# MLP of a two-layer decoder: weight blocks placed behind the features, eight loaded at once, sums and row scaling moved earlier

## The chip, the cores and the metric

The kernel runs on one core of a Trainium2 chip. The metric is the device time of one execution in microseconds (us), and the number quoted for a kernel is the median of several runs. TensorE (PE) does the matmuls, VectorE (DVE), ScalarE (ACT) and GpSimd (POOL) the elementwise work. SyncE (SP) and POOL issue the DMAs that bring weights from HBM; a DMA issued by POOL can add to what lies in its target instead of replacing it (here: accumulating DMA).

## The reference

A decoder trunk of two layers over 512 rows of width 1024, in float32. Layer 0 mixes rows with gated linear attention, layer 1 with stick-breaking attention; behind each mixer stand a norm, an MLP of width 4096 and another norm. Cut to what matters:

```python
def sq_relu_mlp(x, w_up, w_down):
    h = jax.nn.relu(x @ w_up)
    return (h * h) @ w_down

for layer in range(2):
    mix = gla_mixer(h, ...) if layer == 0 else stick_breaking_attention(...) @ sb_w_o
    h = layer_norm(ALPHA * h + mix, ln_g[layer, 0], ln_b[layer, 0])
    h = layer_norm(ALPHA * h + sq_relu_mlp(h, mlp_w_up[layer], mlp_w_down[layer]),
                   ln_g[layer, 1], ln_b[layer, 1])
```

`layer_norm` takes a row's mean and variance, then multiplies by a gain vector `ln_g` and adds a bias vector `ln_b`.

## The kernel before

**Precision.** Every float32 operand is split into a rounded part `hi` (written by ACT, L70 for weights and L98 for features) and the rest `lo` (DVE, L72 and L99). A product takes three matmuls: hi·hi, hi·lo, lo·hi. So each weight block of 128x1024 costs one ACT and one DVE instruction before PE can use it.

**Seven products.** Each 2x2 block product is done with seven block products instead of eight. This needs sums of features (`T`, `tmp` and `s`, DVE lines L725, L840 and L855) and sums of weight blocks. Half of the block sums come for nothing, as accumulating DMAs on POOL (L748, `Blocks.more`); the rest are a DVE addition (L773, `Blocks.sum`) or a DMA of one block onto another (POOL, L771).

**The stages.** The mixer of layer 0 ends in its output projection, the generator `seven` (L341 and on, matmuls at L392). It gives back control after each finished row tile, and `finish` norms that tile: mean and variance on DVE (L177, L182), reciprocal root on POOL (`ve`, `rs`, L183 and L184), centring on DVE (L190), transposes on PE (L267) and the gain and bias in the transposed form on ACT (L270). Four row tiles `h304` to `h307` hold the residual rows. Then `mlp(0, ...)` runs, then the values' projection and the attention of layer 1, its projection `project`, and `mlp(1, ...)`, which ends in the last norm and the store.

**The MLP.** The width of 4096 is cut into four chunks (`NC`). A chunk is an `up` half of seven steps (matmuls at L922, 256 columns each) and a `down` half of seven steps (L973, 512 columns). An object `Step` holds a step's weight blocks and feature operand; `run_all` makes both two steps ahead. `between()` runs inside a step after its matmuls are issued, and is where the next steps' operands are written. `read` takes a step's result from PSUM: in an up step by an ACT copy (L933) or a DVE sum (L938), in a down step by the DVE sums of `Rows.add` (L167, L169). `AHEAD` lists a half's eight weight blocks (four, each in two halves `h`): two plain ones and two that also get an accumulating DMA.

**The first up of an MLP.** Its first two steps use plain pieces (`raw`), loaded ahead. Of its eight blocks, four (layer 0: with their accumulating DMAs) are loaded on SP before the first row tile is normed, and the last four are loaded by POOL (L895) in `rest()`, behind a small POOL copy `pin` (L956) that reads the last row tile's `rs`. In layer 1 two of the accumulating DMAs are issued there too. So POOL's order there is: last `rs`, `pin`, those, then the loads.

**Rows' scaling.** The residual rows get gain and bias on their own, off the path: `times` (L199, DVE, by `lng`) for the four tiles during steps 4 and 5 of the first up and steps 0 and 1 of the first down, `plus` (L202) during the second up. `lng` and `lnb` are loaded on SP by `lnvec` before the output projection in layer 0, and before `finish` in layer 1.

**What sets the order.** Each engine runs its queue in program order. A scheduler places the instructions; those in `keep(...)` (`tc.keep_in_program_order`) stay where the code has them. A load into a pool's slot waits until the former use of that memory is over. In the MLP's pool the block slots (tag `B`) lie at the bottom, where layer 0 had gating tiles and layer 1 the attention's query and key tiles, and the feature tiles (tag `s2`) above them.

Of the kernel before, what the change touches and what calls it, by code (L numbers as in the profile page):

```python
# [8 lines left out]
F32 = mybir.dt.float32  # L9
# [25 lines left out]
def yoco_kernel(ctx: ExitStack, tc: tile.TileContext, x, gla_w_in, gla_w_a2, gla_b_a, gla_norm_g,  # L35
# [298 lines left out]
    def seven(a1, a2, weights, pool, hs, fresh, norms=(), mid=None, begun=None):  # L334
# [9 lines left out]
        bs = []  # L344
# [8 lines left out]
        for h in range(2):  # L353
            four_b = []
            for k, j, other in ((1, 1, (0, 1)), (0, 1, (0, 0)), (0, 0, None), (1, 0, None)):
                b = pool.tile([P, 1024], F32, tag="B", bufs=8, name=nm("B"))
                nc.sync.dma_start(out=b.rearrange("p (a b) -> p a b", a=2), in_=weights(k, h, j))
                if other:
                    more(b, h, *other)
                four_b.append(b)  # L360
            bs.append(four_b)

        def split_b(i):
            got = []
            for h in range(2):
                hi, lo = split_tile(bs[h][i], 2)
# [42 lines left out]
        third = split_a(s1), split_b(1)  # L409
# [303 lines left out]
    vec, vcols = lnvec(0, 0), lncols(0, 0)  # L713
# [79 lines left out]
    def mlp(l, hT, late, vec, done, ready=None):  # L793
# [11 lines left out]
        def operand(a, apart=False):  # L805
# [5 lines left out]
            else:  # L811
                us = [unit(F32R)]
                put(us[0][:, :, LO], us[0][:, :, HI], a)
# [6 lines left out]
        def steps(a11, a12, a21, a22, weights, part, read, order, by=(), plain=None, ops=None, after=None, late_sums=False):  # L820

            made, t = [], []
            hold = keep if after else lambda ins: ins

            def blocks(k=0, j=0, first=False, sums=None):
                def make():
                    if first and not made:
                        made.append(Blocks(mlp_, weights, order, by))
# [6 lines left out]
                    return made[0].pieces(k, j, keep if after and (k, j) == (0, 1) else lambda ins: ins)  # L835
# [22 lines left out]
            makes = [lambda: operand(a11()), lambda: operand(a12()), sum3, sum4, sum5, sum6, lambda: operand(a22())]  # L858
# [19 lines left out]
            def step(n):  # L878
                banks, opens, closes, (i, j), first, make = table[n]

                def go(between=lambda: None):
                    for s in part(me.a, me.b, banks, opens, closes, n):
                        if s == 1:
                            between()
                        yield from read(s, banks, i, j, first, n)

                me = Step(go, make, makes[n])
                if after and n == 0:

                    def rest():  # L890
                        after()
                        if late_sums:
                            for h in range(2):
                                made[0].more(made[0].b[1, 1], (0, 1), h, keep)
                        made[0].load(AHEAD[:2], lambda **to: keep(nc.gpsimd.dma_start(**to)))  # L895

                    me.rest = rest
                if after and n == 3:
# [640 lines left out]
```

## Time and profile before

| what | value |
|---|---|
| median of 3 runs | 1125.41 us (1121.54 to 1128.05) |
| the profiled execution's own time | 1123.68 us |
| its span | 1122.0 us |
| PE busy | 1090.2 us (97%) |
| DVE busy | 903.0 us (80%) |
| ACT busy | 669.7 us (60%) |
| POOL busy | 179.6 us (16%) |
| read from HBM | 176.52 MB, 160 GB/s over the span |
| mean granted clock of PE | 0.991 |

Time outside the span is 1.7 us. Row formats in what follows: a line of the timeline gives start, duration (both in us), engine, line, operation, output<-input, shape, count, and in brackets the time that the engine stood idle just before and what ended it. A line of the table by stages gives, for one stretch, each engine's busy time, then PE's granted clock (1.00 is full), the busy share of the 16 DMA engines and GB/s. Stretches of the run: the output projection of layer 0 from 155 to 218 us, its MLP to about 525, values and attention to about 735, the second projection to 785, the last MLP to 1122.

### The profile page before, as it was taken

Reading aid. Unit: us, or ns where it says so; the run is one execution under the profiler, and the core shown is the slowest. Engines: PE = TensorE matmul, PEld = TensorE weight load, DVE = VectorE, ACT = ScalarE, POOL = GpSimd, SP = SyncE. Lnnn points to the kernel's source line nnn. Section 1 sums busy time; section 2 is a strip of 40 time slices with the busy share of each in tenths; the row PEclk is TensorE's granted clock in tenths of the full one; section 3 lists DMA queues with packets and bytes.
Section 4 is the critical chain, followed back from the end, with each engine's and each line's share of the span. In section 5 each row is a group of like instructions: output and inputs, shape, how many; then the busy total and the mean of one; then the engine's idle time right before and its main releaser. Section 6 shows DMA issues by size and latency. Waiting matters only on the chain. (4 is left out here: it accounts for less than half of the span.)

```text
span 1122.0 us, 16726 instructions
## 1 busy us (share of the span) xinstructions
PE 1090.2 (97%) x6463; PEld 940.2 (84%) x6463; DVE 903.0 (80%) x1087; ACT 669.7 (60%) x963; POOL 179.6 (16%) x213
## 2 busy tenths in 40 slices
PE   9999999999899999999899999999898999999997
PEld 7888878898698898897688777788896998988985
DVE  4488638988989878878887896688789889788787
ACT  4455426676467466565674776776675565574654
POOL 1011210312102101111204001212211022011012
PEclk9999999999999999999999999999899999999998
DMA  7262394778859949866748425356987699599483
GB/s 221 73 187 64 118 240 124 187 226 231 218 148 229 232 144 245 205 171 149 219 83 213 125 76 127 101 111 169 244 208 215 148 247 228 139 221 235 145 223 75
DMA packets 120867, 195.43 MB, mean 174 GB/s; under 512 B 13978, under 2 KB 38938, under 8 KB 120788
## 3 DMA queue, kind: packets, MB, share of 16 engines
q1 hardware_dynamic: 90580, 127.78, 35.4%
q0 software_dynamic: 27744, 61.87, 30.3%
q10 hardware_dynamic: 2464, 4.72, 1.2%
q8 instruction: 51, 0.84, 0.3%
q14 instruction: 28, 0.23, 0.1%
HBM read 176.52 MB, written 3.15 MB: 160 GB/s over the span
## 5 line engine op out<-in xcount | busy, mean ns | idle before, releaser
L72 DVE TENSOR_TENSOR lo<-B,hi 128x1024 fp32r<-128x1024 f32 x206 | 247.3, 1220 | 71.9 <-ACT hi L70 69.6
L70 ACT ACTIVATE hi<-B 128x1024 fp32r<-128x1024 f32 x206 | 212.9, 1054 | 154.2 <-DVE B L773 73.5
L973 PE MATMUL ps<-hi,T 128*128 128x512 f32 x896 | 281.3, 391 | 7.9 <-ACT T L98 3.9
L922 PE MATMUL ps<-T,hi 128*128 128x256 f32 x1280 | 235.6, 286 | 5.1 <-DVE T L99 3.9
L922 PEld LDWEIGHTS ps<-T,hi 128*128 128x128 f32 x1280 | 201.9, 194 | 8.7 <-DVE T L99 4.9
L973 PEld LDWEIGHTS ps<-hi,T 128*128 128x128 f32 x896 | 167.4, 188 | 47.2 <-DVE T L99 5.6
L922 PE MATMUL ps<-T,lo 128*128 128x256 f32 x640 | 181.1, 286 | 1.0 <-DVE lo L72 1.0
L973 PE MATMUL ps<-lo,T 128*128 128x512 f32 x448 | 174.9, 391 | 2.4 <-DVE lo L72 2.4
L922 PEld LDWEIGHTS ps<-T,lo 128*128 128x128 f32 x640 | 123.2, 194 | 2.1 <-DVE lo L72 1.9
L70 ACT ACTIVATE hi<-raw 128x1024 fp32r<-128x1024 f32 x88 | 91.1, 1057 | 45.2 <-PE ps L94 9.3
L72 DVE TENSOR_TENSOR lo<-raw,hi 128x1024 fp32r<-128x1024 f32 x86 | 102.8, 1217 | 18.0 <-ACT hi L70 17.6
L973 PEld LDWEIGHTS ps<-lo,T 128*128 128x128 f32 x448 | 84.2, 188 | 20.8 <-DVE lo L72 4.1
L922 PE MATMUL ps<-A,hi 128*128 128x256 f32 x512 | 93.1, 284 | 0.6 <-ACT hi L70 0.6
L922 PEld LDWEIGHTS ps<-A,hi 128*128 128x128 f32 x512 | 80.1, 192 | 0.8 <-ACT hi L70 0.8
L93 PE MATMUL ps<-T,hi 128*128 128x512 f32 (+1 forms) x200 | 79.7, 399 | 0.4 <-DVE k L99 0.4
L98 ACT ACTIVATE T<-s 128x1024 fp32r<-128x1024 f32 (+1 forms) x52 | 51.5, 994 | 46.6 <-DVE s L855 39.2
L748 POOL DMA_DIRECT2D B<-in_mlp_w_down_dram x32 | 38.5, 1203 | 244.6 <-DVE lo L72 103.5
L95 PE MATMUL ps<-T,lo 128*128 128x512 f32 (+1 forms) x200 | 76.5, 383 | 0.0
L94 PE MATMUL ps<-T,hi 128*128 128x512 f32 (+1 forms) x200 | 76.3, 382 | 0.0
L169 DVE TENSOR_TENSOR h<-h,ps 128x512 f32<-128x512 f32 x108 | 71.0, 679 | 1.7 <-PE ps L973 1.7
L922 PE MATMUL ps<-A,lo 128*128 128x256 f32 x256 | 72.2, 284 | 0.0
L99 DVE TENSOR_TENSOR T<-s,T 128x1024 fp32r<-128x1024 f32 (+1 forms) x52 | 59.2, 1138 | 6.7 <-ACT T L98 6.7
(234 smaller groups left out, 1888.0 us busy)
## 6 DMA issues: line engine op xcount, KB each, us to landing
B<-in_mlp_w_down_dram SPq DMA_DIRECT2D x64, 512.0 KB, 5.2
B<-in_mlp_w_up_dram SPq DMA_DIRECT2D x56, 512.0 KB, 4.9
B<-in_mlp_w_up_dram POOLq DMA_DIRECT2D x40, 512.0 KB, 9.3
B<-in_mlp_w_down_dram POOLq DMA_DIRECT2D x32, 512.0 KB, 9.4
raw<-in_mlp_w_up_dram SPq DMA_DIRECT2D x24, 512.0 KB, 4.6
B<-B POOLq DMA_DIRECT2D x24, 512.0 KB, 5.3
raw<-in_gla_w_in_dram SPq DMA_DIRECT2D x20, 512.0 KB, 3.7
raw<-in_mlp_w_down_dram SPq DMA_DIRECT2D x16, 512.0 KB, 8.9
```

The costliest lines, as they stand in the source:

```text
L70: keep(nc.scalar.activation(hi, raw, AF.Copy))
L72: keep((on or nc.vector).tensor_tensor(lo, raw, hi.bitcast(F32), op=ALU.subtract))
L93: keep(nc.tensor.matmul(ps, lhsT=a[0], rhs=b[0], start=first, stop=False))
L94: keep(nc.tensor.matmul(ps, lhsT=a[0], rhs=b[1], start=False, stop=False))
L95: keep(nc.tensor.matmul(ps, lhsT=a[1], rhs=b[0], start=False, stop=last))
L98: keep(nc.scalar.activation(hi, ps, AF.Copy))
L99: keep((on or nc.vector).tensor_tensor(lo, ps, hi.bitcast(F32), op=ALU.subtract))
L169: nc.vector.tensor_tensor(h, h, ps, op=op)
L748: keep(nc.gpsimd.dma_start(out=got[h].rearrange("p (a b) -> p a b", a=2), in_=self.w(other[0], h, other[1]), accum_op=ALU.add))
L922: nc.tensor.matmul(to, lhsT=b[k][x][:, fs], rhs=a(k)[:, y], start=opens and f % 2 == 0 and (k, x, y) == (0, 0, LO), stop=closes and (k, x) ...
L973: nc.tensor.matmul(banks[s], lhsT=a(k)[:, x][:, P * s:P * s + P], rhs=b[k][y], start=opens and (k, x, y) == (0, LO, 0), stop=closes and (k ...
```

## The change

1. `seven` allocates and loads its eight blocks in the order in which the products use them (`b11`, then `b22`, `b21`, `b12`, both halves each), instead of one half after the other. The splits of the third product (`b12`) are kept in program order.
2. In the MLP's pool the two feature tiles of the first chunk come first (`sq0`), so that the block slots lie behind them, over other former tiles: in layer 0 blocks of the output projection, in layer 1 the attention's work tiles. The mask `low` moves to another pool.
3. The first up's eight blocks are all loaded on SP when they are made, those with accumulating DMAs first. `rest()`, `pin` and the POOL loads of L895 are gone; all four accumulating DMAs of a layer are issued among the norms' POOL work.
4. Both halves of the first block sum (L773) are done in `between()` of step 0, that is during the last tile's norm. Step 0's ACT copies are kept in order at step 1's `between()`.
5. The four `times` come at steps 2, 4, 5 and 6 of the first up, none in the down half. `lng` and `lnb` are loaded in `run_all`, behind the eight blocks.
6. Two operands are pinned in program order: that of `a22` in the first up, and that of `a11` in the downs of later chunks.

The diff, cut to its core (the line numbers of the changed kernel differ a little: L348 for L347 and so on, L922 becomes L920, L840 L843, L855 L858, L938 L937):

```diff
-        for h in range(2):
-            four_b = []
-            for k, j, other in ((1, 1, (0, 1)), (0, 1, (0, 0)), (0, 0, None), (1, 0, None)):
-                b = pool.tile([P, 1024], F32, tag="B", bufs=8, name=nm("B"))
+        for i in (2, 3, 0, 1):
+            for h in range(2):
+                bs[h][i] = pool.tile([P, 1024], F32, tag="B", bufs=8, name=nm("B"))
+        for i, k, j, other in ((2, 0, 0, None), (0, 1, 1, (0, 1)), (3, 1, 0, None), (1, 0, 1, (0, 0))):
+            for h in range(2):
+                b = bs[h][i]
                 nc.sync.dma_start(out=b.rearrange("p (a b) -> p a b", a=2), in_=weights(k, h, j))
                 if other:
                     more(b, h, *other)
...
-        third = split_a(s1), split_b(1)
+        third = split_a(s1), split_b(1, keep=tc.keep_in_program_order)
...
-    vec, vcols = lnvec(0, 0), lncols(0, 0)
+    vcols = lncols(0, 0)
...
+        sq0 = [four(), four()]
...
-                        made.append(Blocks(mlp_, weights, order, by))
+                        made.append(Blocks(mlp_, weights, AHEAD[2:] + AHEAD[:2] if first_up else AHEAD, by))
...
-                        yield from read(s, banks, i, j, first, n)
+                        if first_up and n == 0:
+                            me.read = lambda: read(s, banks, i, j, first, n)
+                        else:
+                            yield from read(s, banks, i, j, first, n)
...
-                    def rest():
-                        after()
-                        if late_sums:
-                            for h in range(2):
-                                made[0].more(made[0].b[1, 1], (0, 1), h, keep)
-                        made[0].load(AHEAD[:2], lambda **to: keep(nc.gpsimd.dma_start(**to)))
-
-                    me.rest = rest
-                if after and n == 3:
-                    me.sum = lambda: (minus_a11(), made[0].sum((0, 0), (1, 1), 0))
+                if first_up and n == 3:
+                    me.sums = lambda: [made[0].sum((0, 0), (1, 1), h) for h in range(2)]
+                    me.minus = minus_a11
...
-                if also and n >= (4 if c == 0 else 1):
+                if also and n in ((2, 4, 5, 6) if c == 0 else (1, 2, 3, 4)):
                     also.pop(0)()
...
+                if n == 0:
+                    vec.extend(lnvec(l, 0))
 
                 def between():
                     if n == 0:
-                        step.rest()
+                        todo[3].sums()
                     if n == 1:
+                        todo[0].read()
                         todo[2].make_operand()
-                        todo[3].sum()
+                        todo[3].minus()
```

What it moves. **POOL, start of layer 1's MLP.** Names are tiles with a running number; `B` are weight blocks, `ve` and `rs` the norm's steps for one row tile. Before, from the last tile's `rs` on:

```order
L184 TENSOR_TENSOR rs_7510<-ve_7509,mhalf 128x1
L956 COPY pin_7605<-rs_7510 128x1
L748 DMA B_7525<-in_mlp_w_up_dram 128x2x512
L748 DMA B_7527<-in_mlp_w_up_dram 128x2x512
L895 DMA B_7609<-in_mlp_w_up_dram 128x2x512
L895 DMA B_7611<-in_mlp_w_up_dram 128x2x512
L895 DMA B_7613<-in_mlp_w_up_dram 128x2x512
L895 DMA B_7615<-in_mlp_w_up_dram 128x2x512
L771 DMA B_7613<-B_7609 128x1024
L771 DMA B_7615<-B_7611 128x1024
```

After, from the first accumulating DMA on:

```order
L748 DMA B_7515<-in_mlp_w_up_dram 128x2x512
L748 DMA B_7518<-in_mlp_w_up_dram 128x2x512
L748 DMA B_7521<-in_mlp_w_up_dram 128x2x512
L183 TENSOR_SCALAR ve_7356<-mv_7355 128x1
L184 TENSOR_TENSOR rs_7357<-ve_7356,mhalf 128x1
L748 DMA B_7524<-in_mlp_w_up_dram 128x2x512
L183 TENSOR_SCALAR ve_7377<-mv_7376 128x1
L184 TENSOR_TENSOR rs_7378<-ve_7377,mhalf 128x1
L183 TENSOR_SCALAR ve_7448<-mv_7447 128x1
L184 TENSOR_TENSOR rs_7449<-ve_7448,mhalf 128x1
L183 TENSOR_SCALAR ve_7503<-mv_7502 128x1
L184 TENSOR_TENSOR rs_7504<-ve_7503,mhalf 128x1
```

The four loads of L895 and the copy `pin` are gone, three accumulating DMAs stand ahead of the first tile's norm and one between the first and second tile's.

**DVE, same place.** Before, from the last tile's centring (L190) on; `T` and `tmp` are features and their sums, `lo` the second part of a split:

```order
L190 TENSOR_SCALAR h_1641<-h_1641,mv_7508,rs_7510 128x1024
L72 TENSOR_TENSOR lo_7492<-raw_7488,hi_7490 128x1024
L72 TENSOR_TENSOR lo_7531<-B_7519,hi_7529 128x1024
L72 TENSOR_TENSOR lo_7535<-B_7522,hi_7533 128x1024
L840 TENSOR_TENSOR tmp_7689<-T_7222,T_7221 128x1024
L938 TENSOR_TENSOR s_7617<-s_7617,ps_7621 128x2x256
L938 TENSOR_TENSOR s_7617<-s_7617,ps_7622 128x2x256
L99 TENSOR_TENSOR T_7691<-tmp_7689,T_7691 128x4x256
L725 SCALAR_TENSOR_TENSOR tmp_7689<-tmp_7689,T_7221 128x1024
L773 TENSOR_TENSOR B_7609<-B_7609,B_7525 128x1024
L725 SCALAR_TENSOR_TENSOR T_7222<-T_7222,tmp_7689 128x4x256
L99 TENSOR_TENSOR T_7696<-tmp_7689,T_7696 128x4x256
```

After:

```order
L190 TENSOR_SCALAR h_1641<-h_1641,mv_7502,rs_7504 128x1024
L72 TENSOR_TENSOR lo_7486<-raw_7482,hi_7484 128x1024
L72 TENSOR_TENSOR lo_7537<-B_7515,hi_7535 128x1024
L72 TENSOR_TENSOR lo_7541<-B_7518,hi_7539 128x1024
L773 TENSOR_TENSOR B_7527<-B_7527,B_7521 128x1024
L773 TENSOR_TENSOR B_7529<-B_7529,B_7524 128x1024
L843 TENSOR_TENSOR tmp_7687<-T_7220,T_7219 128x1024
L937 TENSOR_TENSOR s_7513<-s_7513,ps_7617 128x2x256
L99 TENSOR_TENSOR T_7689<-tmp_7687,T_7689 128x4x256
L937 TENSOR_TENSOR s_7513<-s_7513,ps_7618 128x2x256
L725 SCALAR_TENSOR_TENSOR tmp_7687<-tmp_7687,T_7219 128x1024
L725 SCALAR_TENSOR_TENSOR T_7220<-T_7220,tmp_7687 128x4x256
```

Both block sums (L773) stand ahead of the feature sum `tmp`, where one stood behind `tmp` and the other further on, and the first `T` split (L99) stands one row earlier among the sums of `s`.

**DVE, first down half of layer 1.** Before, from step 0's row sum on:

```order
L167 SCALAR_TENSOR_TENSOR h_1639<-h_1639,ps_8088 128x512
L99 TENSOR_TENSOR T_8071<-tmp_8069,T_8071 128x4x256
L199 TENSOR_TENSOR h_1640<-h_1640,lng_7223 128x1024
L773 TENSOR_TENSOR B_7965<-B_7965,B_7979 128x1024
L725 SCALAR_TENSOR_TENSOR tmp_8069<-tmp_8069,s_7617 128x1024
L169 TENSOR_TENSOR h_1638<-h_1638,ps_8117 128x512
L72 TENSOR_TENSOR lo_8106<-B_7965,hi_8104 128x1024
L773 TENSOR_TENSOR B_7967<-B_7967,B_7982 128x1024
L99 TENSOR_TENSOR T_8114<-tmp_8069,T_8114 128x4x256
L169 TENSOR_TENSOR h_1639<-h_1639,ps_8131 128x512
L72 TENSOR_TENSOR lo_8111<-B_7967,hi_8109 128x1024
L199 TENSOR_TENSOR h_1641<-h_1641,lng_7223 128x1024
```

After, from the last `times` (L199) on:

```order
L199 TENSOR_TENSOR h_1641<-h_1641,lng_7543 128x1024
L72 TENSOR_TENSOR lo_8061<-B_7970,hi_8059 128x1024
L843 TENSOR_TENSOR tmp_8067<-s_7514,s_7513 128x1024
L72 TENSOR_TENSOR lo_8065<-B_7973,hi_8063 128x1024
L167 SCALAR_TENSOR_TENSOR h_1638<-h_1638,ps_8072 128x512
L99 TENSOR_TENSOR T_8069<-tmp_8067,T_8069 128x4x256
L167 SCALAR_TENSOR_TENSOR h_1639<-h_1639,ps_8086 128x512
L773 TENSOR_TENSOR B_7962<-B_7962,B_7976 128x1024
L725 SCALAR_TENSOR_TENSOR tmp_8067<-tmp_8067,s_7513 128x1024
L169 TENSOR_TENSOR h_1638<-h_1638,ps_8114 128x512
L72 TENSOR_TENSOR lo_8103<-B_7962,hi_8101 128x1024
L773 TENSOR_TENSOR B_7964<-B_7964,B_7979 128x1024
```

Two instructions of L199 are gone from among the block sums and `T` splits; one of them stands ahead of `tmp` now, and a row sum (L167) came in behind the first `T` split.

More of the change, by code (lines that the diff above doesn't have):

```diff
@@ L791, in make_operand, with mlp @@
             self.a = self.operand()
-    def mlp(l, hT, late, vec, done, ready=None):
+    def mlp(l, hT, late, done, ready=None):
         ml = tc.tile_pool(name=nm("mlp"), bufs=1, reuse_waits="tile")
@@ L812, in operand @@
                 us = [unit(F32R)]
-                put(us[0][:, :, LO], us[0][:, :, HI], a)
+                put(us[0][:, :, LO], us[0][:, :, HI], a, **how)
             return views(us)
@@ L818, in views, with steps @@
             return lambda k: us[k // n][:, k % n, :]
-        def steps(a11, a12, a21, a22, weights, part, read, order, by=(), plain=None, ops=None, after=None, late_sums=False):
+        def steps(a11, a12, a21, a22, weights, part, read, by=(), plain=None, ops=None, held=()):
             made, t = [], []
-            hold = keep if after else lambda ins: ins
+            first_up = bool(plain)
+            hold = keep if first_up else lambda ins: ins
             def blocks(k=0, j=0, first=False, sums=None):
@@ L834, in make @@
                         return made[0].plain(1, 1)
-                    return made[0].pieces(k, j, keep if after and (k, j) == (0, 1) else lambda ins: ins)
+                    return made[0].pieces(k, j, hold if (k, j) == (0, 1) else lambda ins: ins)
                 return make
@@ L928, in read @@
                 if n == 0:
-                    sq.extend([four(), four()])
+                    sq.extend([four(), four()] if c else sq0)
+                hold = lambda ins: ins if c or n else keep(ins)
                 for s in range(2):
@@ L947, in up, with down @@
             if c:
-                made = steps(*(None,) * 4, w, part, read, AHEAD, ops=ops)
+                made = steps(*(None,) * 4, w, part, read, ops=ops)
             else:
                 plain = [ready[:4], ready[4:]] if ready else [pieces_512(mlp_w_up[l], 512 * k, 4, 0) for k in range(2)]
-                last = hs[3].rs
-                first = (AHEAD[2], AHEAD[3] if l == 0 else (1, 1, None))
-                def after():
-                    nc.gpsimd.tensor_copy(out=small(1, "pin"), in_=last)
-                made = steps(r[0], r[2], r[1], r[3], w, part, read, first, ((1, 0),), plain, ops, after,
-                             l == 1)
+                made = steps(r[0], r[2], r[1], r[3], w, part, read, ((1, 0),), plain, ops, (6,))
             return made, [lambda s=s, j=j: sq[j][:, :, s] for j in range(2) for s in (LO, HI)]
-        def down(c, q, norms=(), by=(), also=()):
+        def down(c, q, norms=(), by=(), held=()):
             w = lambda k, h, j: block(mlp_w_down[l], 1024 * c + 512 * k + 256 * h, 512 * j)
             seen = set()
-            also = list(also)
             def part(a, b, banks, opens, closes, n):
@@ L981, in read @@
                 seen.add((i, j, s))
-                if also and s == 1 and n < 2:
-                    also.pop(0)()
                 if norms and n > 3:
                     yield (s, ~s, 2 + s)[n - 4]
-            return steps(q[0], q[2], q[1], q[3], w, part, read, AHEAD, by)
+            return steps(q[0], q[2], q[1], q[3], w, part, read, by, held=held)
+        vec = []
         turns = [lambda h=h: h.times(vec, keep) for h in hs]
@@ L1154, in done0 @@
         return values(y, late, bs)
-    held = mlp(0, hT, late, vec, done0)
+    held = mlp(0, hT, late, done0)
     sbx = tc.tile_pool(name="sb", bufs=1, reuse_waits="tile")
     sbp = sbx.__enter__()
-    low = tri(sbp, "low", F32, 0.0, -1.0e30, [[-1, P]], ALU.is_gt, 1)
+    low = tri(const, "low", F32, 0.0, -1.0e30, [[-1, P]], ALU.is_gt, 1)
     def chain():
```

24 lines of the change are left out of this document (10 added, 14 removed).

## The prediction

> **What bounds the kernel now.** I read the page first, then the table by stages, then the timelines of PE and DVE where a stage falls short. The page gives the share of each engine.
>
> ```profile
> span 1122.0 us, 16726 instructions
> PE 1090.2 (97%) x6463; PEld 940.2 (84%) x6463; DVE 903.0 (80%) x1087; ACT 669.7 (60%) x963; POOL 179.6 (16%) x213
> ```
>
> PE is the bound at 97%, and the change takes no matmul away. So all that can be won is PE's idle time and the time in which its clock is low. The table by stages shows where that lies.
>
> ```profile
> core 0: us, PE busy (x) PEld busy (x) DVE busy (x) ACT busy (x) POOL busy (x), PEclk, DMA share, GB/s
> 160.00:180.00 20.00, 20.00 (x90) 16.41 (x89) 8.35 (x12) 8.74 (x12) 1.71 (x2) 0.93 0.72 157
> 200.00:220.00 20.00, 19.57 (x96) 15.70 (x95) 19.55 (x28) 11.87 (x25) 7.62 (x9) 1.00 0.71 175
> 220.00:240.00 20.00, 19.42 (x163) 19.02 (x161) 14.91 (x18) 15.54 (x29) 6.38 (x10) 1.00 0.94 262
> 280.00:300.00 20.00, 16.83 (x70) 12.37 (x69) 20.00 (x21) 11.01 (x12) 2.69 (x3) 1.00 0.78 211
> 320.00:340.00 20.00, 20.00 (x169) 20.00 (x168) 18.39 (x18) 14.32 (x17) 2.12 (x2) 1.00 0.42 135
> 800.00:820.00 20.00, 17.30 (x116) 16.49 (x115) 17.42 (x18) 13.97 (x18) 1.81 (x2) 0.83 0.64 181
> 840.00:860.00 20.00, 17.10 (x73) 12.99 (x72) 20.00 (x21) 8.15 (x8) 1.76 (x2) 1.00 0.83 225
> ```
>
> A later chunk (320 to 340) has PE busy for 20.00 of 20: nothing is to be had there. The change touches three kinds of place: the output projection (200 to 220: PE 19.57 and DVE 19.55 of 20, both full), the start of each MLP (220 to 240 and 800 to 820) and the first down half of each (280 to 300 and 840 to 860, DVE 20.00, PE down to 16.83 and 17.10). I go through them from the last.
>
> **Start of layer 1's MLP: -5.0.** PE's timeline shows four waits and then slow matmuls; DVE's and POOL's show why.
>
> ```profile
> 795.56 0.39 PE L922 MATMUL ps<-T,hi 128*128 128x256 f32 x1 [1.50 <-DVE T L99]
> 802.61 0.39 PE L922 MATMUL ps<-T,hi 128*128 128x256 f32 x1 [1.27 <-ACT hi L70]
> 803.79 0.50 PE L922 MATMUL ps<-T,hi 128*128 128x256 f32 x2 [0.79 <-DVE T L99]
> 804.93 0.58 PE L922 MATMUL ps<-T,lo 128*128 128x256 f32 x1 [0.63 <-DVE lo L72]
> 805.74 0.41 PE L922 MATMUL ps<-T,lo 128*128 128x256 f32 x1
> 805.95 0.41 PE L922 MATMUL ps<-T,hi 128*128 128x256 f32 x1
> 811.35 0.28 PE L922 MATMUL ps<-T,lo 128*128 128x256 f32 x1
> 811.47 0.40 PE L922 MATMUL ps<-T,hi 128*128 128x256 f32 x2
> ...
> 791.19 1.23 DVE L840 TENSOR_TENSOR tmp<-T,T 128x1024 f32<-128x1024 f32 x1 [1.27 <-ACT T L270]
> 793.68 0.69 DVE L938 TENSOR_TENSOR s<-s,ps 128x512 f32<-128x512 f32 x1 [0.67 <-PE ps L922]
> 794.29 1.22 DVE L99 TENSOR_TENSOR T<-tmp,T 128x1024 fp32r<-128x1024 f32 x1
> 800.24 1.23 DVE L773 TENSOR_TENSOR B<-B,B 128x1024 f32<-128x1024 f32 x1 [3.48 <-DMA B<-in_mlp_w_up_dram]
> ...
> 781.68 0.55 POOL L183 TENSOR_SCALAR ve<-mv 128x1 f32<-128x1 f32 x1 [6.92 <-DVE mv L182]
> 787.75 3.96 POOL L895 DMA_DIRECT2D B<-in_mlp_w_up_dram  x4
> ```
>
> DVE stands 3.48 us in the block sum L773, because the block whose load POOL issues at 787.75 has not landed before 800.2, 12.4 us later. Behind it in DVE's queue stand the `T` split and the `lo` that PE then waits for: 1.27 + 0.79 + 0.63 = 2.69 us idle. And from 804.93 on PE starts a matmul each 0.21 us (805.74 to 805.95) where it later needs 0.12 (811.35 to 811.47). If that holds up to about 811, 6.1 us / 0.21 = 29 matmuls lost 0.09 each: 2.6. After the change all eight blocks are issued by SP, from when the attention's work tiles are free, tens of us ahead of use; so both go: -5.3. What comes in: both L773 now stand ahead of `tmp`. DVE is idle 1.27 before `tmp`, two additions take 2 x 1.14 (a start each 1.14 us, as 1.22 overlaps), so `tmp` moves from 791.2 to 792.2, 1.0 later. But the first `T` split, for which PE waits 1.50, stood behind two sums `s`, the second of them held by PE; it stands ahead of that one now. Its earliest time is `tmp` 792.2, + 2.3 for the sum and ACT's half, + the rest: 794.6 where it was 794.29. So this wait grows by 0.3. The accumulating DMAs on POOL go before and between the norm's steps; POOL is idle there for 6.92 before the third tile's `ve` (781.68), so I cost them at 0. Sum: -5.3 + 0.3 = -5.0. Between 0 (the blocks come late in another way) and -6.5 (the 1.50 goes too) I take the value in which only what the POOL loads caused goes.
>
> **First down half, both layers: -1.7 each.** DVE has no gap there and PE waits for it.
>
> ```profile
> 282.95 0.73 PE L973 MATMUL ps<-hi,T 128*128 128x512 f32 x2 [1.09 <-DVE T L99]
> 290.31 0.50 PE L973 MATMUL ps<-hi,T 128*128 128x512 f32 x1 [1.94 <-ACT T L98]
> ...
> 834.40 0.69 DVE L167 SCALAR_TENSOR_TENSOR h<-h,ps 128x512 f32<-128x512 f32 x1 [1.38 <-PE ps L973]
> 838.67 1.23 DVE L72 TENSOR_TENSOR lo<-B,hi 128x1024 fp32r<-128x1024 f32 x1 [0.86 <-ACT hi L70]
> 841.55 1.22 DVE L199 TENSOR_TENSOR h<-h,lng 128x1024 f32<-128x1024 f32 x1
> 842.69 1.22 DVE L773 TENSOR_TENSOR B<-B,B 128x1024 f32<-128x1024 f32 x1
> 850.70 1.22 DVE L199 TENSOR_TENSOR h<-h,lng 128x1024 f32<-128x1024 f32 x1
> ...
> 849.10 0.73 PE L973 MATMUL ps<-hi,T 128*128 128x512 f32 x2 [0.90 <-DVE T L99]
> 856.46 0.50 PE L973 MATMUL ps<-hi,T 128*128 128x512 f32 x1 [1.93 <-ACT T L98]
> ```
>
> Two L199 (841.55, 850.70) stand in the full stretch, ahead of the `T` split and of L725, on which the two waits of PE rest. Each costs 1.14 of DVE's time, 2.28 together. They move to steps 2 and 6, the latter into the idle 1.38 before 834.40 and 0.86 before 838.67: cover enough for 1.14. In exchange the order shows a row sum L167 that now falls behind the first `T` split, into the full stretch: + 0.6. So -1.7, and what is left of 0.90 + 1.93 = 2.83 is about 1.1. Layer 0 has the same pattern with 1.09 and 1.94 and the same order, so again -1.7. Bounds: 0 (if step 6's L199 delays `tmp` instead) and -2.3 each.
>
> **Start of layer 0's MLP: -0.9.**
>
> ```profile
> 230.07 1.23 DVE L840 TENSOR_TENSOR tmp<-T,T 128x1024 f32<-128x1024 f32 x1 [3.42 <-ACT T L270]
> 243.67 0.51 PE L922 MATMUL ps<-A,hi 128*128 128x256 f32 x2 [0.55 <-ACT hi L70]
> 244.52 0.39 PE L922 MATMUL ps<-T,lo 128*128 128x256 f32 x1 [0.34 <-DVE lo L72]
> ```
>
> The two L773 go into the 3.42 us in which DVE waits before `tmp`, and out of the full stretch behind it. That should take the waits of 0.55 and 0.34: -0.9. The cover is thin: the second L773 needs a load and an accumulating DMA that have to come by 228. From about 200 on, eight loads, four accumulating DMAs and one `raw` piece, 13 x 524 KB, must land; at 262 GB/s (the row of 220 to 240) one takes 2.0, all 26 us, up to 226. That is an estimate with some 2 us to spare; late, it holds `tmp` and PE one for one. Bounds -1.5 and +3.
>
> **Output projection: 0.** PE waits once here, and runs slow after it.
>
> ```profile
> 157.56 0.83 PE L679 MATMUL ps<-ident,h 128*128 128x128 f32 x4 [2.03 <-DVE h L672]
> 185.91 1.22 DVE L408 TENSOR_TENSOR T<-T,T 128x1024 f32<-128x1024 f32 x1
> 209.89 0.81 DVE L190 TENSOR_SCALAR h<-h,mv,rs 128x1024 f32<-128x1024 f32 x1 [0.19 <-POOL rs L184]
> ...
> 207.19 0.93 SPq L736 DMA_DIRECT2D B<-in_mlp_w_up_dram  x2
> ```
>
> The wait of 2.03 is a block that lands late and holds ACT, with the gating behind it; the new order loads that block earlier. The clock of 0.93 in 160 to 180 is 7% of 20, another 1.4: PE is some 3.5 earlier. DVE's L408 comes earlier with it (185.91 to about 182.4). But the pinned splits of the third product move five `lo` from before L408 to behind it, against two `lo` of `raw` that move behind the first centring: 3 x 1.14, and up to a fourth piece, 3.4 to 4.6 more between L408 and the first L190. As DVE is full there, the first L190 stays near 209.9, and PE waits for it later instead. So 0, between -3.5 and +3 (the norm's POOL steps now have accumulating DMAs between them, 1.3 us of issue each).
>
> **Sum.** -5.0 - 1.7 - 1.7 - 0.9 + 0 = -9.3. The profiled execution took 1123.7 (1.7 outside its span), 0.15% under the median 1125.4 of the runs, which spread by 0.6%; so 1114.4 from the one and 1116.1 from the other: I say 1115. No change that can be told is within 0.5%, 5.6 us (1119.8 to 1131).
>
> **Two rules of the Trainium skill.** The matmuls' slow stretch at 804.93 follows 2.69 us of waits within 4 us, while the wait of 1.93 at 856.46 leaves the clock at 1.00 in its stage, and that of 2.03 at 157.56 is followed by a stage with 0.93. The Trainium skill, "TensorE: Matmul & The Clock Gate", section "HAM oscillation — how this bites in real kernels", gives as rule no idle gaps above about 3.4 us; by it alone all these waits would leave the clock as it is. The trace does not agree: shorter waits already did. By the row of 157.56 my remaining wait of 1.8 in layer 1 could cost 1.4 more, by those of 795.56 and 856.46 nothing; I take nothing. The other rule speaks against the change, and stands at the second rival.
>
> **Rivals.** *The projection's gain comes through* (0.13): if DVE's queue is shorter than my count, the 3.5 us reach the MLP: 1111.5. For it: DVE is at 8.35 of 20 in 160 to 180; against: 19.55 in 200 to 220. *Late transfers in layer 0* (0.27): the 13 transfers push the `raw` piece of the first step, the second L773 and POOL's norm steps 2 to 4 us back, and one idle stretch of 2 us brings 1.4 of slow clock, as at 157.56; +5: 1120. The DMA share of 0.94 in 220 to 240 speaks for it, the 3.42 us of cover against. The Trainium skill, "DMA: Bandwidth & Descriptors", section "Issuing engines are not separate DMA queues", says that another issuing engine saves only the issue and that all transfers share the same 16 engines; by that, moving eight loads to SP wins only where they start earlier. The 12.4 us of layer 1 against the 0.94 of layer 0 agree as far as they go. *The waits only move* (0.11): the loads of layer 1 start no earlier, as SP, in order, stands behind another load that waits for DVE; then only the down halves gain, -3.4: 1121. *Slower* (0.09): POOL, in order, stands at an accumulating DMA whose block's load waits for its slot, while `rs` of the next tiles are behind it. Each us after about 216 for the fourth block then delays a tile's norm, L270 and PE by as much, with 1.4 to 2.6 of slow clock on top. With the other gains kept, the loss must pass 16 to show as slower; a block that lands at 231 would do it: 1132. Against: SP issued the last such loads at 207 before, and one takes some 2 to 12 us.
>
> **Numbers.** Forecast 0.40 at 1115, within 1110 to 1119 if no rival holds. Low 1107 takes in the projection's gain and the -6.5; high 1122 the two cases about 1120. Faster by over 0.5%: forecast 0.40, the projection 0.13 and a third of late transfers 0.09: 0.62. Within 0.5%: 0.18 of late transfers and the 0.11: 0.29. Slower 0.09.
>
> **What would show it.** In the changed profile: no DVE wait before L773 at the start of layer 1's MLP, PE's clock near 1.00 there instead of 0.83; PE busy about 18.2 to 18.5 of 20 in both first down halves; the wait at 157 gone but the first MLP starting within 1 us of before. Wrong would prove me a DVE wait before the second L773 or `rs` held on POOL at 215 to 225, a new idle stretch of PE near 205 to 220 with a low clock behind it, or a first `T` split in layer 1 well after 795.

## The result

The changed kernel takes 1116.46 us (median of 9 runs, 1114.35 to 1118.94), the kernel before 1122.26 us (9 runs, 1121.18 to 1128.05) in the same comparison: a ratio of 0.9938, with a 95% interval of 0.9920 to 0.9956. The ratio is taken over all runs of both and gives 7.0 us or 0.6% (the two medians lie 5.8 apart). The sum of the prediction was -9.3 and its time 1115, so sign and size came out near; the parts of the sum did not, as the rest shows.

The page of the changed kernel, in the rows that answer to those of before:

```profile
span 1114.8 us, 16712 instructions
PE 1086.1 (97%) x6463; PEld 940.0 (84%) x6463; DVE 903.4 (81%) x1087; ACT 668.1 (60%) x963; POOL 172.3 (15%) x203
```

The table by stages of the changed kernel, the same columns:

```profile
160.00:180.00 20.00, 20.00 (x95) 16.48 (x94) 5.69 (x9) 6.55 (x9) 1.67 (x2) 1.00 0.63 156
200.00:220.00 20.00, 18.70 (x94) 14.89 (x93) 18.64 (x28) 9.66 (x22) 7.95 (x10) 1.00 0.90 252
240.00:260.00 20.00, 16.96 (x141) 16.76 (x140) 18.86 (x20) 16.15 (x20) 2.75 (x3) 1.00 0.60 175
260.00:280.00 20.00, 19.70 (x103) 17.52 (x104) 18.47 (x19) 11.91 (x14) 2.97 (x3) 0.91 0.97 227
280.00:300.00 20.00, 20.00 (x90) 16.58 (x89) 20.00 (x22) 12.53 (x13) 3.27 (x3) 1.00 0.78 222
800.00:820.00 20.00, 16.27 (x135) 16.02 (x134) 18.37 (x20) 15.60 (x20) 2.91 (x3) 1.00 0.52 164
820.00:840.00 20.00, 20.00 (x106) 17.76 (x105) 18.45 (x19) 11.39 (x14) 2.75 (x3) 0.91 0.97 232
840.00:860.00 20.00, 20.00 (x92) 16.65 (x91) 20.00 (x22) 12.73 (x14) 3.73 (x4) 1.00 0.75 229
```

The old holes (280 to 300, 840 to 860, the clock of 0.83 in 800 to 820) are gone. A new one stands two stages ahead of each of the two down-half holes: PE is busy for 16.96 and 16.27 of 20 in 240 to 260 and 800 to 820, and the clock is 0.91 in the next stage. PE's and DVE's timelines of the changed kernel show it:

```profile
260.30 0.80 PE L963 MATMUL ps<-hi,T 128*128 128x512 f32 x1 [3.33 <-ACT T L98]
819.40 0.50 PE L963 MATMUL ps<-hi,T 128*128 128x512 f32 x1 [3.73 <-ACT T L98]
...
814.14 1.28 DVE L937 TENSOR_TENSOR s<-s,ps 128x512 f32<-128x512 f32 x2
815.34 1.22 DVE L199 TENSOR_TENSOR h<-h,lng 128x1024 f32<-128x1024 f32 x1
816.47 2.35 DVE L72 TENSOR_TENSOR lo<-B,hi 128x1024 fp32r<-128x1024 f32 x2
818.74 0.68 DVE L937 TENSOR_TENSOR s<-s,ps 128x512 f32<-128x512 f32 x1
819.38 1.22 DVE L99 TENSOR_TENSOR T<-s,T 128x1024 fp32r<-128x1024 f32 x1
```

PE waits 3.33 and 3.73 us at the first matmul of the first down half (L963) for the pinned operand's split `T`. (This pin stands in the down half of each layer's first chunk, `() if c else (0,)`; "the downs of later chunks" in part 6 of the change is a slip.) DVE has no idle time in the rows around it: it works without a stop from 249.4 to 265 and from 808.5 to 824.

For the parts I compare where PE starts a step, read from its timeline as the start of the step's first matmul (us from the span's start; in brackets the distance from the row above):

```
                          before           changed          unpinned (e1)    scaling only (e2)
first up, layer 0         218.79           217.60           217.62           215.86
its third step            232.75 (13.96)   232.52 (14.92)   232.55 (14.93)   229.83 (13.97)
first down, second step   270.36 (37.61)   273.10 (40.58)   272.07 (39.52)   268.27 (38.44)
its seventh step          305.14 (34.78)   303.05 (29.95)   303.21 (31.14)   300.12 (31.85)
first up, layer 1         779.35           776.08           775.17           774.27
its fifth step            813.13 (33.78)   803.99 (27.91)   803.08 (27.91)   807.08 (32.81)
first down, second step   836.70 (23.57)   832.23 (28.24)   829.86 (26.78)   831.30 (24.22)
its seventh step          871.29 (34.59)   862.18 (29.95)   861.00 (31.14)   862.45 (31.15)
```

Layer 1 wins 5.9 up to its fifth step, loses 4.7 up to the down half's second step, and wins 4.6 after that: 5.8 in all. Layer 0 wins 0.9 over the same stretch (86.35 to 85.45).

### The profile page after: what moved, and what is told of

It reads as the page before. It is cut to its first block, busy times and chain, and to the rows that moved or that the text cites. A ratio compares the mean times of both kernels' runs of the same rounds, so it can differ in the third digit from the quotient of the medians.

```text
span 1114.8 us, 16712 instructions
## 1 busy us (share of the span) xinstructions
PE 1086.1 (97%) x6463; PEld 940.0 (84%) x6463; DVE 903.4 (81%) x1087; ACT 668.1 (60%) x963; POOL 172.3 (15%) x203
## 5 line engine op out<-in xcount | busy, mean ns | idle before, releaser
L963 PE MATMUL ps<-hi,T 128*128 128x512 f32 x896 | 280.8, 391 | 9.9 <-ACT T L98 7.1
L920 PE MATMUL ps<-T,hi 128*128 128x256 f32 x1280 | 235.9, 286 | 4.3 <-DVE T L99 2.8
L920 PEld LDWEIGHTS ps<-T,hi 128*128 128x128 f32 x1280 | 202.2, 194 | 8.0 <-DVE T L99 3.6
L963 PEld LDWEIGHTS ps<-hi,T 128*128 128x128 f32 x896 | 168.1, 188 | 47.5 <-ACT T L98 7.5
L920 PE MATMUL ps<-T,lo 128*128 128x256 f32 x640 | 180.9, 285 | 0.0
L963 PE MATMUL ps<-lo,T 128*128 128x512 f32 x448 | 174.8, 390 | 2.0 <-DVE lo L72 1.9
L920 PEld LDWEIGHTS ps<-T,lo 128*128 128x128 f32 x640 | 123.3, 194 | 0.3
L963 PEld LDWEIGHTS ps<-lo,T 128*128 128x128 f32 x448 | 84.2, 188 | 19.5 <-DVE lo L72 2.7
L920 PE MATMUL ps<-A,hi 128*128 128x256 f32 x512 | 92.5, 283 | 0.0
L920 PEld LDWEIGHTS ps<-A,hi 128*128 128x128 f32 x512 | 79.9, 192 | 0.0
L920 PE MATMUL ps<-A,lo 128*128 128x256 f32 x256 | 72.4, 283 | 0.0
L99 DVE TENSOR_TENSOR T<-s,T 128x1024 fp32r<-128x1024 f32 (+1 forms) x52 | 59.2, 1139 | 3.9 <-ACT T L98 3.9
```

Source lines behind the costliest of these rows:

```text
L99: keep((on or nc.vector).tensor_tensor(lo, ps, hi.bitcast(F32), op=ALU.subtract))
L920: nc.tensor.matmul(to, lhsT=b[k][x][:, fs], rhs=a(k)[:, y], start=opens and f % 2 == 0 and (k, x, y) == (0, 0, LO), stop=closes and (k, x) ...
L963: nc.tensor.matmul(banks[s], lhsT=a(k)[:, x][:, P * s:P * s + P], rhs=b[k][y], start=opens and (k, x, y) == (0, LO, 0), stop=closes and (k ...
```

## The experiments

All ratios are to the kernel before, run beside it on the same chip. Rows can come from different chips, so compare ratios, not medians.

| kernel | median us | ratio | interval |
|---|---|---|---|
| changed | 1116.46 | 0.9938 | 0.9920 to 0.9956 |
| e1 changed, operand not pinned | 1113.02 | 0.9913 | 0.9896 to 0.9929 |
| e2 before + scaling moved | 1116.95 | 0.9945 | 0.9926 to 0.9965 |
| e3 before + projection's part | 1126.02 | 1.0034 | 1.0020 to 1.0048 |
| e5 changed, pin a step earlier | 1116.09 | 0.9942 | 0.9924 to 0.9961 |
| e6 changed, old projection | 1118.44 | 0.9972 | 0.9959 to 0.9985 |
| e7 before + block part | 1118.17 | 0.9956 | 0.9938 to 0.9975 |
| e8 changed, no scaling | 1109.61 | 0.9889 | 0.9875 to 0.9904 |
| e9 changed, old projection, not pinned | 1116.39 | 0.9950 | 0.9938 to 0.9962 |
| e10 as e1, scaling on POOL | 1126.97 | 1.0044 | 1.0026 to 1.0063 |
| e11 changed, scaling at old places | 1116.41 | 0.9944 | 0.9925 to 0.9963 |
| e12 as e1, third split free | 1118.04 | 0.9969 | 0.9950 to 0.9987 |
| e13 as e9, block part in layer 1 alone | 1111.90 | 0.9904 | 0.9887 to 0.9920 |

**e1: the pin taken away.**

```diff
-            todo += down(c, q, ..., ((1, 0),), () if c else (0,))
+            todo += down(c, q, ..., ((1, 0),), ())
```

> The changed kernel, with the first down's operand a11 no longer pinned in program order (one argument; everything else as changed). Theory A, the pin holds: the T split of that operand stands behind ACT's squares of a later step, and PE waits 3.4 us (layer 0) and 3.8 us (layer 1) at the start of the first down, with some 1.8 us of lower clock behind each; without the pin both go and at most 1.1 us of DVE time comes back in each: 7 to 9.5 us under the changed kernel, about 1108, ratio to before 0.985 to 0.989. Rival B, DVE is full there and the pin only decides where PE waits: the T split moves up, something else behind it moves down by the same 2 to 4 us: 1114 to 1118, ratio 0.992 to 0.996.

Measured 0.9913, between the two theories: the interval reaches into B's range and not into A's. The profile is that of B: PE still waits at the first down half in both layers, 2.00 us a few matmuls further on and with another releaser, and the clock is still low after it. PE's timeline, and the row of the stage, of e1:

```profile
259.66 0.50 PE L963 MATMUL ps<-lo,T 128*128 128x512 f32 x1 [2.00 <-DVE lo L72]
817.43 0.80 PE L963 MATMUL ps<-lo,T 128*128 128x512 f32 x1 [2.00 <-DVE lo L72]
810.00:830.00 20.00, 18.00 (x115) 16.28 (x114) 17.92 (x19) 14.15 (x16) 4.79 (x4) 0.91 0.94 211
```

From the first up's start to the seventh step of the down half the two kernels take the same: 85.45 and 85.59 in layer 0, 86.10 and 85.83 in layer 1. So the pin does not make the loss; it sets where PE waits and for what. What the 0.25% are by which e1 is the better is open (e9 is by 0.22% better than e6, where the same pin is the only difference); the profile has them in no one place, and the intervals of e1 and the changed kernel overlap.

**e5: the pin a step earlier.**

```diff
+                    if n == 4:
+                        todo[7].make_operand()
...
```

> The changed kernel, where the first down's operand a11 is still kept in program order but written one step earlier (in the fourth step's between() instead of the fifth's). Theory A: ACT gets to it before the squares of step 4, so PE's wait at the start of the down half goes, as without the pin: 1106 to 1110. Rival B, DVE is the limit: 1114 to 1118.

Measured 0.9942, as the changed kernel: B.

**e2: the scaling alone.**

```diff
-                if also and n >= (4 if c == 0 else 1):
+                if also and n in ((2, 4, 5, 6) if c == 0 else (1, 2, 3, 4)):
...
-            made, q = up(c, turns[:2] if c == 0 else plus if c == 1 else ())
+            made, q = up(c, turns if c == 0 else plus if c == 1 else ())
```

> The kernel before, with only the row scaling moved: the four times (L199) at steps 2, 4, 5, 6 of the first up, none in the first down. Theory (the prediction's term): -1.7 us for each layer's first down half, -3.4 in all, ratio 0.997; the waits of PE at the third and fourth step of that half shrink from 2.9 to about 1.1 together. Rival: the step 6 scaling delays the first feature sum of the down half and nothing is won: ratio 1.000.

Measured 0.9945, 6.2 us: nearly as much as the whole change. The table of steps gives 2.9 in layer 0's down half from its second to its seventh step (34.78 to 31.85) and 3.4 in layer 1's. Ahead of that layer 0 loses 0.8 and layer 1 wins 0.3, so that from the first up on 2.1 and 3.8 are won. In the down half of layer 0 PE is busy for 19.37 of 20 where it had 16.83:

```profile
280.00:300.00 20.00, 19.37 (x96) 16.18 (x97) 20.00 (x22) 11.66 (x12) 3.62 (x3) 1.00 0.82 234
```

This profile also has the first up 2.9 us earlier, at 215.86 against 218.79. That is not from the edit: the wait of 2.03 at 157 is simply not there in this run, and the projection starts 2.9 earlier (174.60 against 177.53). Up to there PE, ACT, DVE and POOL have the same instructions in the same order in both. PE's timeline of e2 has the same transposes (L679) with no idle time in front:

```profile
156.48 0.60 PE L679 MATMUL ps<-ident,h 128*128 128x128 f32 x4
```

**e3: the projection alone.**

> The kernel before, with only the output projection's block order and its kept third split. Theory (the prediction's term): PE's wait of 2.0 us near 157 and the low clock behind it go, but DVE's queue gives it back before the first MLP: 0, that is ratio 0.999 to 1.001. Rival: two thirds of it reach the MLP, as the comparison of the two traces has it (first up 2.1 us earlier, counted from the projection's start): ratio 0.998; with all of it 0.997.

Its edit is part 1 of the change, on the kernel before:

```diff
-        for h in range(2):
-            four_b = []
-            for k, j, other in ((1, 1, (0, 1)), (0, 1, (0, 0)), (0, 0, None), (1, 0, None)):
+        for i, k, j, other in ((2, 0, 0, None), (0, 1, 1, (0, 1)), (3, 1, 0, None), (1, 0, 1, (0, 0))):
+            for h in range(2):
...
-        third = split_a(s1), split_b(1)
+        third = split_a(s1), split_b(1, keep=tc.keep_in_program_order)
```

Measured 1.0034, 3.8 us slower, on neither side of what I expected. Against a run without the wait at 157 (e2) the projection starts as early (174.8 and 174.6), and the first up starts 2.0 later (217.90 and 215.86). From the projection's first matmul to the first up it is 43.1 us in e3 and in the changed kernel, 41.3 in e2 and before. DVE's timeline in e3 is full from 198 up to the wait for the first `rs`, and the first centring is where it was before, though the projection starts 2.7 earlier:

```profile
206.11 1.28 DVE L169 TENSOR_TENSOR h<-h,ps 128x512 f32<-128x512 f32 x2
207.31 1.28 DVE L177 BATCH_NORM_STATS2 bst<-h 128x6 f32<-128x512 f32 x2
209.73 0.81 DVE L190 TENSOR_SCALAR h<-h,mv,rs 128x1024 f32<-128x1024 f32 x1 [0.36 <-POOL rs L184]
```

**e7, e6, e9, e12: the block part and the projection.** e7 is the kernel before with parts 2, 3 and 4 of the change and, of part 5, the later loads of `lng` and `lnb`. e6 is the changed kernel without part 1 (the diff of e3 backwards), e9 the same without the first down's pin too (as e1). e12 is e1 with one argument less:

```diff
-        third = split_a(s1), split_b(1, keep=tc.keep_in_program_order)
+        third = split_a(s1), split_b(1)
```

> The kernel before with only the block part: slots behind the features, eight loads on SP, both first sums at the last tile's norm; projection, row scaling and pins as before. The prediction's terms: -5.0 and -0.9, so 1116, ratio 0.995. If the parts just add up (scaling 0.9945, projection 1.0034, all without the pin 0.9913): 0.9934, 1114.6. Rival, DVE is full from the first sums to the fourth down step, so that what PE gains at the start it waits for at the down half: the start of layer 1 shows -8 to -10, the end of the first down half -3 to -4, ratio 0.997.

> The changed kernel with the output projection's blocks loaded in the old order and its third split unpinned again; all else as changed. Theory A: the new order costs some 3.8 us (it made the kernel before 0.34% slower when alone), so about 1112.7, ratio to before 0.990. Rival B: it cost only because the kernel before has no wait at 157 in most runs, while in the changed kernel the later waits hide it: 1116, ratio 0.994.

> The changed kernel with both the old projection and the unpinned first down operand. If the costs of the two (0.34% and 0.25%) add up: ratio 0.988, about 1109. Rival, DVE is the limit at the down half, so that whatever comes earlier waits there: not better than the unpinned one alone, 0.991.

> The changed kernel without the pin of the first down's operand, and with the projection's third split left to the scheduler, which puts four of its lo (two of the third product, two of the fourth) ahead of the feature sum L408 again. Theory: the pinned split costs the 1.9 us by which the first MLP starts late against a projection without a wait at 157; free, these come back: 1111, ratio 0.990. Rival: the pin is what frees the slots for the MLP's blocks in time; without it the first sums wait for a load as with the old order: 1114 to 1117.

Measured: e7 0.9956, e6 0.9972, e9 0.9950, e12 0.9969. So the projection's part, which costs 3.8 us alone, is worth some 4 us in the company of the block part (0.9972 to 0.9938, 0.9950 to 0.9913): both theories of e6 are wrong, e9 is slower than either of its figures, and by e12 the pinned split is what counts. e12's first up does start 2.1 earlier than e1's (215.52 against 217.62), as its theory has it, but the time is a little worse than its rival's. DVE's and PE's timelines show what happens; the first four rows are of e7, then two of e12, then two of the changed kernel:

```profile
224.58 1.23 DVE L774 TENSOR_TENSOR B<-B,B 128x1024 f32<-128x1024 f32 x1 [1.22 <-DMA B<-in_mlp_w_up_dram]
229.33 1.23 DVE L774 TENSOR_TENSOR B<-B,B 128x1024 f32<-128x1024 f32 x1 [3.52 <-DMA B<-in_mlp_w_up_dram]
230.47 1.22 DVE L844 TENSOR_TENSOR tmp<-T,T 128x1024 f32<-128x1024 f32 x1
232.84 0.50 PE L921 MATMUL ps<-T,hi 128*128 128x256 f32 x2 [2.94 <-ACT T L98]
```

```profile
229.30 1.22 DVE L773 TENSOR_TENSOR B<-B,B 128x1024 f32<-128x1024 f32 x1 [3.26 <-DMA B<-in_mlp_w_up_dram]
232.81 0.79 PE L920 MATMUL ps<-T,hi 128*128 128x256 f32 x2 [3.28 <-ACT T L98]
```

```profile
227.89 2.35 DVE L773 TENSOR_TENSOR B<-B,B 128x1024 f32<-128x1024 f32 x2
230.16 1.22 DVE L843 TENSOR_TENSOR tmp<-T,T 128x1024 f32<-128x1024 f32 x1
```

Without the new order or its pinned split, the second block sum of layer 0 stands 3.0 to 3.5 us for a load, `tmp` behind it, and PE behind that, with slow matmuls after it. In the changed kernel the sum waits for nothing. But the block does not come earlier there: by the traces the fourth accumulating DMA lands at 228.7 in the changed kernel, 229.3 in e12 and e7, 229.9 and 230.2 in e9 and e6, although the changed kernel issues its last three loads only at 213 to 214 and the others all eight by 208. The DMA engines are full all the while in both of the rows below (215 to 230, changed kernel, then e12); what differs is that DVE has work to do:

```profile
215.00:230.00 15.00, 13.66 (x104) 12.57 (x103) 13.23 (x18) 13.40 (x32) 3.50 (x6) 1.00 1.08 292
215.00:230.00 15.00, 14.15 (x116) 13.63 (x114) 8.13 (x12) 9.60 (x22) 3.53 (x5) 1.00 1.10 287
```

So e12's reason, that the pin frees the slots in time, is not borne out. With the pin PE starts the first up later and reaches the late block without a long wait; without it PE starts earlier, waits 3.28 and then runs slow (its third step takes 9.0 us in e12, 6.9 in the changed kernel). By the down half's seventh step e12 is 2.3 us behind e1 (305.53 against 303.21); where the rest of the difference between their ratios lies is open.

In all of them the second sum starts at 229 to 230 and the third step of the first up at 232.5 to 233.7. With the old loads the third step starts at 229.83 (e2). Up to the fifth step that shrinks: 243.86 in e2, 245.28 in the changed kernel, 246.74 in e7. So in these profiles the early loads bring layer 0 no lead; it stands 1.4 to 2.9 us behind.

In layer 1 the block part alone takes PE from the first up's start to the seventh step of the down half in 85.29 us (before 91.94): 6.7 won. It gives nothing back at the first down half (fifth step to second down step 23.91, before 23.57), so e7's rival is not borne out there. The scaling alone wins 3.8 (88.18). Together with the pin off they win 6.1 (85.83), not 10.4. The rows of that stretch, of the kernel before, e2, e7 and the changed kernel, show why:

```profile
779.35:871.29 91.94, 83.90 (x521) 74.57 (x520) 80.33 (x86) 60.53 (x79) 19.24 (x21) 0.96 0.79 211
774.27:862.45 88.18, 81.45 (x522) 73.66 (x520) 80.28 (x87) 60.20 (x79) 20.44 (x22) 0.98 0.82 220
775.43:860.72 85.29, 80.12 (x522) 71.70 (x522) 80.07 (x85) 60.32 (x80) 14.37 (x15) 1.00 0.76 200
776.08:862.18 86.10, 80.14 (x521) 73.61 (x520) 80.38 (x86) 60.42 (x80) 14.37 (x15) 0.98 0.73 199
```

DVE (the third busy time) has the same 80 us of work in all four. What the parts take away is its idle time: 11.6 us before, 7.9 with the scaling moved, 5.2 with the block part, 5.7 with both. The block part alone leaves the scaling no idle time to win.

**e8, e11, e10: who gives it back.** e8 leaves out the four row multiplications of each layer, e11 puts them back to their old places, e10 gives them to POOL:

```diff
(e8)
-            made, q = up(c, turns if c == 0 else plus if c == 1 else ())
+            made, q = up(c, () if c == 0 else plus if c == 1 else ())
(e11)
-                if also and n in ((2, 4, 5, 6) if c == 0 else (1, 2, 3, 4)):
+                if also and n in ((4, 5) if c == 0 else (1, 2, 3, 4)):
...
+                if also and s == 1 and n < 2:
+                    also.pop(0)()
(e10)
-            keep(nc.vector.tensor_tensor(self.h, self.h, vec[0], op=ALU.mult))
+            keep(nc.gpsimd.tensor_tensor(self.h, self.h, vec[0], op=ALU.mult))
```

> The changed kernel without the four row multiplications of each layer (L199 left out, so the residual rows miss the gain lng). Theory A, DVE is the limit from the first up's third step to the first down's fourth: without 4 x 1.14 us of its work the wait at the first down's start shrinks from 3.4 and 3.8 us to under 1, and the end of the first down half comes 3 to 5 us earlier in each layer: 1107 to 1110, ratio 0.986 to 0.989. Rival B, the pin alone makes the wait: it stays at 3 us or more, and not more than 1 us is won per layer: 1114 to 1116.

> The changed kernel with the row scaling at its old places (up steps 4 and 5, down steps 0 and 1); all else as changed, pin included. Theory, one full stretch of DVE: the wait at the first down's start shrinks by what the two L199 ahead of it take (2.3 us), and the two waits later in the down half come back (0.9 to 2.3 us each): within 2 us of the changed kernel, ratio 0.992 to 0.996. Rival, the terms add up: without the scaling's 5 to 6 us it stands at 1121 to 1122, ratio 0.999.

> The changed kernel without the pin of the first down's operand, and with the four row multiplications of each layer on POOL instead of DVE, at the same places in the code. Theory, DVE is the limit there: 4.6 us less work of DVE in each layer, as when they were left out (-4.9 us from the changed kernel with the pin), and the pin's 2.8 too as far as a wait is left: 1106 to 1109, ratio 0.985 to 0.988. Rival: POOL's multiplication (some 2.4 us each, from its split at line 72) stands ahead of accumulating DMAs in POOL's queue and delays the block sums of the down half: ratio 0.990 to 0.994.

Measured: e8 0.9889, in theory A's range. PE's wait ahead of the first down half is 1.2 and 1.1 us, still with the pin (it stands before the up half's seventh step, which comes first in e8):

```profile
258.51 0.48 PE L920 MATMUL ps<-T,hi 128*128 128x256 f32 x2 [1.19 <-DVE s L937]
813.64 0.47 PE L920 MATMUL ps<-T,hi 128*128 128x256 f32 x2 [1.12 <-DVE s L937]
```

So the wait is mostly DVE's amount of work, theory A, though not under 1 us as it had it. e11, 0.9944, is the changed kernel again: where in this stretch the four multiplications stand does not matter once the block part is in. A part of PE's wait stands early, and a part late, at the down half's fifth step as before:

```profile
258.94 0.50 PE L964 MATMUL ps<-hi,T 128*128 128x512 f32 x1 [2.11 <-ACT T L98]
817.06 0.50 PE L964 MATMUL ps<-hi,T 128*128 128x512 f32 x1 [1.28 <-ACT T L98]
288.75 0.50 PE L964 MATMUL ps<-hi,T 128*128 128x512 f32 x1 [1.48 <-ACT T L98]
846.87 0.50 PE L964 MATMUL ps<-hi,T 128*128 128x512 f32 x1 [1.44 <-ACT T L98]
```

e10, 1.0044, is worse than both theories. Its timelines of POOL, ACT and DVE:

```profile
266.61 5.22 POOL L199 TENSOR_TENSOR h<-h,lng 128x1024 f32<-128x1024 f32 x2
271.86 2.01 ACT L70 ACTIVATE hi<-B 128x1024 fp32r<-128x1024 f32 x2 [7.49 <-POOL h L199]
272.95 2.36 DVE L72 TENSOR_TENSOR lo<-B,hi 128x1024 fp32r<-128x1024 f32 x2 [8.50 <-ACT hi L70]
```

`lng` lies in one of the eight slots of the tag `hi`. The next split into that slot may not begin before the last L199 has read it, and on POOL, behind its accumulating DMAs and at 2.6 us each, that is 272. ACT stands 7.49 us, DVE 8.50.

**e13: what the runs point to.** Scaling moved in both layers, the block part in layer 1 alone, the projection's old order, no pins in layer 0 and none on the first down's operand.

```diff
-                        made.append(Blocks(mlp_, weights, AHEAD[2:] + AHEAD[:2] if first_up else AHEAD, by))
+                        made.append(Blocks(mlp_, weights, (AHEAD[2:] + AHEAD[:2] if l else AHEAD[2:]) if first_up else AHEAD, by))
...
-                        todo[3].sums()
+                        todo[3].sums() if l else step.rest()
```

> The scaling moved in both layers, the block part (slots, eight loads, early sums) in layer 1 only; layer 0 with the loads and slots of the kernel before, the projection in its old order, the first down's operand unpinned. Theory: in layer 0 the eight early loads win nothing, since the second sum's blocks land near 229 whatever else is done (with the old loads its third step starts at 229.8 in the scaling-only run against 232.5 to 233.7 in the others), so 2 to 3 us come back against the unpinned changed kernel: 1109 to 1111, ratio 0.988 to 0.990. Rival: the early start is waited for again at the first down half of layer 0, and the result equals the unpinned changed kernel, 0.991 to 0.992.

Measured 0.9904, better than the changed kernel (0.9938; the intervals touch at 0.9920); against e1 (0.9913) the intervals overlap widely, so the theory's 2 to 3 us are not shown by the times. In the profile layer 0 does as in e2 (first up to the down half's seventh step 83.59 us; e1 85.59, e2 84.26).

## Why the prediction was right, point by point

**The total: right.** -9.3 forecast, -7.0 measured (4.9 to 9.0 by the interval), in the range and on the side with the larger chance, though the interval reaches below the 0.5% at which the prediction would call it faster. That the total lies this near is in part luck. In the two profiles layer 1's stretch wins 5.8 (forecast -6.7), layer 0's 0.9 (forecast -2.6), the first up starts 1.2 earlier for a reason that need not be the change's (below), 1.2 come between the layers, and 1.9 are lost after layer 1's first down half, where nothing was forecast. Parts that were priced too low and a wait that was not priced at all offset each other.

**Start of layer 1's MLP, -5.0: right.** From the first up's start to its fifth step PE is 5.9 faster. DVE's wait for the POOL loads is gone, the clock in 800 to 820 went from 0.83 to 1.00, and both sums stand ahead of `tmp` without a wait. Counted from the first up, `tmp` comes 0.9 later (12.78 against 11.84), as forecast; PE's wait of 1.50, which I had growing by 0.3, became two of 0.57 and 0.76:

```profile
786.59 2.36 DVE L773 TENSOR_TENSOR B<-B,B 128x1024 f32<-128x1024 f32 x2
788.86 1.22 DVE L843 TENSOR_TENSOR tmp<-T,T 128x1024 f32<-128x1024 f32 x1
791.21 1.23 DVE L99 TENSOR_TENSOR T<-tmp,T 128x1024 fp32r<-128x1024 f32 x1 [0.53 <-ACT T L98]
```

**The gain that is given back: missing.** The failed step is that the terms were added. I costed each of them against the DVE of before; but in layer 1 DVE has 80 us of work from the first up to the seventh down step whatever the order, and the block part alone brings the stretch down to 85.3. With the scaling's L199 moved ahead, PE waits for DVE at the first down half instead: 3.33 and 3.73 us, with the slow clock behind. The prediction priced the pin of the first down's operand not at all, and looked for this wait nowhere. e8 shows that DVE's work makes most of it, e1 and e5 that without the pin, or with an earlier one, the stretch stays within 0.8 us of its length.

**Down halves, -1.7 each: right mechanism, size too small.** Alone (e2) it is 2.9 and 3.4 from the second to the seventh step. In the steps that I costed, up to the fifth, it is 1.9 and 2.4; the two steps behind (14.83 us from the fifth to the seventh step before, 13.76 in e2) gave another 1.1 that I had not counted. In the changed kernel PE is busy for 20.00 of 20 there, where I had 18.2 to 18.5: the wait had moved ahead.

**Start of layer 0's MLP, -0.9: too large.** The third step starts 14.92 after the first where it took 13.96, so +1.0; by the fifth step, with the waits of 0.55 and 0.34 gone as forecast, it is -0.3 (27.68 against 27.98). The second sum needs its loads until near 229, where I had put 226 to 228; that is the mechanism of the rival "late transfers", which stands openly in e6, e7, e9 and e12.

**Projection, 0: right for another reason.** Counted against the profiled run of before, the first up starts 1.2 earlier. But the wait at 157 is 2.03 in the profile of before and none in e2, with the same program up to there; so my -3.5 rested on the one profile, and the cost of DVE's longer queue, which I had at +3.4 to +4.6, is the one that stays: 1.9 us up to the first up in the profiles, 1.0034 alone. That this pinned split spares the first up its wait for the second sum was not in my working.

**The rule on idle gaps** of the Trainium skill ("TensorE: Matmul & The Clock Gate", section "HAM oscillation — how this bites in real kernels") would have left the clock alone below 3.4 us; the waits of 2.00 in e1 were followed by 0.91. My remark that shorter waits already did so holds. But the length alone does not decide: a wait of 2.00 at the same place in e9 was followed by a stage at 1.00.

```profile
261.69 0.50 PE L964 MATMUL ps<-lo,T 128*128 128x512 f32 x1 [2.00 <-DVE lo L72]
260.00:280.00 20.00, 18.31 (x103) 16.14 (x104) 19.43 (x20) 12.82 (x15) 5.26 (x5) 1.00 1.02 248
```

## What to carry to other kernels

Add the terms of a change only if the engine that hides them has room for all of them: find the stretch in which a second engine is nearly full, take its work there as the floor, and cost the parts inside it together. A wait in one profile of before is a term only if other runs show it too. Run parts both alone and without each other before calling them gain or loss, since a part that loses alone (the projection's pinned split) can gain beside another one.

## What the runs showed of the hardware

POOL took 2.6 us for the 128x1024 multiplication that takes DVE 1.22. Two programs that are the same up to there differ at 157: one waits 2.03 us, with a clock of 0.93 in its stage, the other not at all. In layer 0 the fourth accumulating DMA landed at 228.7 to 230.2 in the changed kernel, e6, e7, e9 and e12, whether the last loads were issued at 206 or at 214; the DMA share from 215 to 230 was 1.08 in the changed kernel and 1.10 in e12. Waits of 2.00 us were followed by a clock of 0.91 over the next stage in e1, and by 1.00 in e9.
